# The last group of a feed-forward block's down projection: pairs 8 and 9 by Strassen's products, pair 10 into their banks, and a mixer's operands half by half

## The chip, the core and the metric

The program runs on one core of one Trainium2 chip. The metric is the device time of one execution in microseconds (us). The kernel before takes 2611.32 us, the median of 3 runs (2610.97 to 2614.04).

Five engines work side by side, each through its own stream of instructions in a fixed order: TensorE (PE; the loads of its stationary operand are shown apart, PEld), VectorE (DVE), ScalarE (ACT), GpSimd (POOL) and SyncE (SP, which issues the transfers). An instruction that waits for another engine holds up all that stand behind it on its own engine. Matmuls add into PSUM banks; the other operands lie in SBUF.

## The reference

T = 512 + 256 = 768 tokens of width 1024 pass through two layers. Each has a feed-forward block (FFN) ahead of and behind its mixer, and a last norm ends the trunk:

```python
def swiglu(h, wg, wu, wd):
    return (jax.nn.silu(h @ wg) * (h @ wu)) @ wd
...
    x = x + 0.5 * swiglu(rmsnorm(x, f1_n), f1_g, f1_u, f1_d)
    x = x + mixer_ab(rmsnorm(x, mix_n), w_in, ...)        # layer 1: mixer_c(..., w_qkv, rpb, w_out)
    x = x + 0.5 * swiglu(rmsnorm(x, f2_n), f2_g, f2_u, f2_d)
...
    return rmsnorm(x, final_norm)
```

Gate and up are 1024x2816, down is 2816x1024, all in float32. `mixer_ab` is a gated unit beside windowed attention, `mixer_c` attention within a 2-D neighbourhood.

## The kernel before

**Operands in two parts.** Every float32 factor is split into a high part, which ScalarE casts, and a low part, which VectorE forms as the factor less the high part. A product is three matmuls (`mm3`, lines 187 to 192): high by high, high by low, low by high. For weights, `wsplit` (111 to 123) writes `whi` (cast, L121) and `wlo` (subtraction, L122) into five buffers each, or, with `keep`, into two of the eight buffers of tag `s`. For activations, `split` (205 to 208) does the same (L207, L208). The weights come as `raw` tiles of 128x1024 float32, in four buffers, by transfers that SP issues in the order of the code.

**The residual** is `self.x[0..7]`: eight rows of 128 channels by 768 tokens. HALVES are tokens 0 to 383 (half 0) and 384 to 767 (half 1). Most matmuls have 384 columns, one half.

**An FFN** (`ffn`, line 475) cuts the 2816 hidden channels into 11 pairs of 128-channel blocks. `pair(p)` computes gate and up for a pair by Strassen's seven products in Winograd's form on a 2x2 cut of weights and tokens, and `hidden` ends with four quarters h11, h12, h21, h22 (block by half). `operands(q)` makes from them the seven right-hand operands b11, t1, b21, t2, t3, b22, n4 of the down projection, each split; for an odd pair the last four steps of it are kept in `self.later`, and `more(n)` takes n of them between the products of `down`.

`down(pre, pairs, d, acc)` (696) multiplies the down weights with these operands, again by seven products, for two pairs at a time: 0 and 1, 2 and 3, 4 and 5, 6 and 7. Each product goes into four banks j = 0 to 3 (128 output channels each). X, Y, Z and W name the four sums: t1 goes to Z, which is added to the four accumulators `acc`; b11 to X, copied by ScalarE into Y ("fork"); b21 ends X, added to x (rows 0 to 3, half 0); t2 goes on in Y, copied into W; t3 gives Y for rows 4 to 7, half 1; b22 ends W for rows 0 to 3, half 1; n4 ends Y for rows 4 to 7, half 0. `sums` (674) makes the four sums of weights s1 to s4 on VectorE, 128x512 each.

The eleventh pair leaves an odd one: pair 8 goes through `down` alone after pair 9's gate and up. While pair 10's gate and up run, `last_operands` (747) splits pair 9's quarters into `dh` and adds each accumulator into its two quarters of x (eight additions, L757). Then `last_operands` splits pair 10's quarters, and `down_last` (761) multiplies pairs 9 and 10 plainly: for each row m four blocks k, two halves, three matmuls, 192 matmuls in all. Its weights come as two rows' columns at a time (4 blocks by 256).

**What follows an FFN** is one of four things, so each FFN has its own tail: first FFN into mixer 0 (`m0`), second into the third FFN (`f`), third into mixer 1 (`m1`), fourth into the last norm (`last`). Where an FFN or the last norm follows (`lag`), `down_last` does half 0 of all rows first, keeps half of the weights' splits, and calls `half_done(0)` between the halves; a mixer gets both halves of a row one after the other. After each addition into x, `final` (792) squares the row for the following norm (L227, L230), and for a mixer, once half 1 of a row is there, makes `xh` (ScalarE, L806) and `xl` (VectorE, L807), the split of x times the norm's gain, which mixer 0 or 1 multiplies in the order of rows 0 to 7. For mixer 1 the tokens are reordered on the way (`columns`), which takes three pieces per row.

**What sets the order.** PE's order is that of the code. The other engines are ordered by a scheduler when the program is built, from the code's order and modelled times. Work beside the main stream (norm steps, feeding the next FFN) runs in generators that are stepped when a modelled PE time is reached; DELAY1 and the arguments of `norm_half` are such delays in us. PSUM has two pools of four banks, `ps_mm` and `ps_aux`, each used in turn.

## Time and profile before

| | before |
|---|---|
| median of 3 runs | 2611.32 us |
| the profiled execution, its time | 2610.36 us |
| its span | 2608.6 us |
| mean granted clock of TensorE | 0.993 |
| PE busy | 2561.0 us (98%), 15114 instructions |
| PEld busy | 2492.0 us (96%) |
| DVE busy | 2249.8 us (86%), 4699 |
| ACT busy | 1369.1 us (52%), 2867 |
| first matmul on `dh` in the four FFNs | 478.59, 1222.34, 1709.69, 2560.34 us |

The profile shows one execution. Busy times are sums over the span, which hides stages of different kinds; so the prediction reads stretches and single rows as well. In an instruction's row stand its start and its duration, the engine, the line of the code, output and inputs, and at the end, where there was one, the idle time before it and what ended it. The four times in the last row mark where the plain products begin, and so where the tails lie.

### The profile page before, as it was taken

What the parts mean: (1) busy time and instruction counts of PE and PEld (TensorE: products, weight loads), DVE (VectorE), ACT (ScalarE), POOL (GpSimd) and SP (SyncE); (2) the same over time, 40 slices, a digit from 0 to 9 for tenths busy, and PEclk for the clock granted to TensorE, in tenths of its full rate; (3) what the DMA queues carried; (4) which work ended last, traced back from release to release, by engine and by line L of the source; (5) the groups of instructions that cost most, each with busy time, mean ns of one, the idle gap of its engine ahead of it and who ended that gap; (6) DMA issues with size and microseconds to landing.
All of it is one profiled execution on the core that took longest, in us unless ns stands there. A gap on an engine that the chain in (4) does not pass through costs nothing.

```text
span 2608.6 us, 41165 instructions
## 1 busy us (share of the span) xinstructions
PE 2561.0 (98%) x15114; PEld 2492.0 (96%) x15114; DVE 2249.8 (86%) x4699; ACT 1369.1 (52%) x2867; POOL 89.8 (3%) x173
## 2 busy tenths in 40 slices
PE   8999999999999999999999999999999999999998
PEld 8999999988899999999999999989898999999997
DVE  8998899888779989889999888986777699888897
ACT  7544454556665545445654445454455475444543
POOL 0000000000100000000000000001222100000000
PEclk9999999999999999999999999999999999999999
DMA  6333222421223322122322222232221322222222
GB/s 217 111 115 92 80 73 65 153 71 52 81 78 97 97 65 77 70 80 83 97 81 81 76 71 73 72 129 63 64 64 40 106 91 96 81 65 81 67 68 77
DMA packets 86201, 221.87 MB, mean 85 GB/s; under 512 B 20464, under 2 KB 33264, under 8 KB 86000
## 3 DMA queue, kind: packets, MB, share of 16 engines
q1 hardware_dynamic: 85712, 218.96, 26.3%
q8 instruction: 118, 1.93, 0.3%
q14 instruction: 83, 0.68, 0.1%
q10 hardware_dynamic: 288, 0.29, 0.1%
HBM read 209.78 MB, written 15.07 MB: 86 GB/s over the span
## 4 chain that ended last, share of the span: by engine, by line
PE 86%; DVE 9%; ACT 2%; issue 1%; DMA 1%; SPq 0%; DVEq 0%; ACTq 0%
PE ps_mm L151 54%; PE ps_aux L151 31%; DVE wlo L122 2%; PE ps_aux L155 1%; DVE s L676 1%; ACT p L1005 1%; DVE xl L807 1%; DMA raw<-in_w 1%; DVE p L999 0%; DVE tl L208 0%; DVE ol L208 0%; DVE u L560 0%; ACT whi L121 0%; ACT xh L806 0%; DVE p L1015 0%
## 5 line engine op out<-in xcount | busy, mean ns | idle before, releaser
L121 ACT CAST whi<-s 128x512 fp32r<-128x512 f32 x496 | 304.8, 621 | 417.6 <-DVE s L676 186.8
L121 ACT CAST whi<-raw 128x512 fp32r<-128x512 f32 x504 | 306.1, 619 | 234.0 <-PE ps_mm L151 94.5
L122 DVE TENSOR_TENSOR wlo<-s,whi 128x512 fp32r<-128x512 f32 x496 | 336.8, 684 | 56.5 <-ACT whi L121 51.1
L122 DVE TENSOR_TENSOR wlo<-raw,whi 128x512 fp32r<-128x512 f32 x486 | 330.7, 688 | 24.0 <-ACT whi L121 17.8
L151 PE MATMUL ps_mm<-db,whi 128*128 128x384 f32 x864 | 219.3, 334 | 0.4 <-DVE sg L569 0.4
L151 PE MATMUL ps_aux<-dt,whi 128*128 128x384 f32 x864 | 219.2, 334 | 0.0
L151 PEld LDWEIGHTS ps_mm<-db,whi 128*128 128x128 f32 x864 | 156.0, 188 | 0.7 <-DVE sg L569 0.7
L151 PEld LDWEIGHTS ps_aux<-dt,whi 128*128 128x128 f32 x864 | 156.0, 188 | 0.0
L151 PE MATMUL ps_mm<-xh,whi 128*128 128x512 f32 (+1 forms) x416 | 147.9, 356 | 4.0 <-ACT xh L806 4.0
L151 PE MATMUL ps_aux<-dt,wlo 128*128 128x384 f32 x432 | 144.4, 334 | 1.4 <-DVE wlo L122 1.4
L151 PE MATMUL ps_mm<-db,wlo 128*128 128x384 f32 x432 | 144.3, 334 | 0.0
L151 PE MATMUL ps_mm<-xl,whi 128*128 128x512 f32 (+1 forms) x416 | 143.0, 344 | 1.1 <-DVE xl L807 1.1
L151 PE MATMUL ps_mm<-xh,wlo 128*128 128x512 f32 (+1 forms) x416 | 142.6, 343 | 0.0
L560 DVE TENSOR_TENSOR u<-ps_aux,u 128x384 f32<-128x384 f32 x176 | 96.8, 550 | 5.4 <-PE ps_aux L151 5.2
L676 DVE TENSOR_TENSOR s<-raw,raw 128x512 f32<-128x512 f32 x124 | 83.9, 684 | 20.3 <-DMA raw<-in_w 20.3
L676 DVE TENSOR_TENSOR s<-raw 128x512 f32<-128x512 f32 x124 | 84.8, 684 | 17.2 <-DMA raw<-in_w 17.0
L151 PE MATMUL ps_aux<-dh,whi 128*128 128x384 f32 x384 | 97.7, 335 | 0.6 <-DVE x L773 0.6
L1005 ACT ACTIVATE p<-p,st 128x256 f32<-128x256 f32 (+3 forms) x144 | 68.9, 480 | 52.8 <-DVE st L1003 52.7
L728 DVE TENSOR_TENSOR x<-ps_aux,x 128x384 f32<-128x384 f32 x160 | 84.7, 550 | 13.7 <-PE ps_aux L151 13.7
L151 PEld LDWEIGHTS ps_mm<-xh,whi 128*128 128x128 f32 x416 | 80.7, 194 | 14.4 <-ACT xh L806 4.9
L151 PE MATMUL ps_mm<-oh,whi 128*128 128x384 f32 x256 | 88.8, 347 | 4.6 <-DVE x L982 4.0
L728 DVE TENSOR_TENSOR x<-ps_mm,x 128x384 f32<-128x384 f32 x160 | 85.7, 550 | 5.8 <-PE ps_mm L151 5.6
(507 smaller groups left out, 8044.4 us busy)
## 6 DMA issues: line engine op xcount, KB each, us to landing
raw<-in_w SPq DMA_DIRECT2D x346, 512.0 KB, 3.6
xdm<-x SPq DMA_DIRECT2D x16, 384.0 KB, 2.3
x<-in_x SPq DMA_DIRECT2D x16, 192.0 KB, 4.7
tok<-in_xt SPq DMA_DIRECT2D x12, 256.0 KB, 6.3
x<-xdm SPq DMA_DIRECT2D x8, 384.0 KB, 4.2
xold<-xdm SPq DMA_DIRECT2D x8, 384.0 KB, 3.0
out_y<-y SPq DMA_DIRECT2D x8, 384.0 KB, 2.4
tab<-skew SPq DMA_DIRECT2D x8, 256.0 KB, 6.6
```

What stands on the lines that cost most here:

```text
L121: nc.scalar.copy(hi, src)
L122: (eng or nc.gpsimd).tensor_tensor(out=lo, in0=src, in1=hi.bitcast(F32), op=ALU.subtract)
L151: self.nc.tensor.matmul(out, lhsT=lhsT, rhs=rhs, start=start, stop=stop, **kw)
L155: self.nc.tensor.transpose(out, src, self.ident)
L560: nc.vector.tensor_tensor(out=t, in0=bank[key, n], in1=t, op=ALU.add)
L676: f = lambda o, x, y, op: self.nc.vector.tensor_tensor(out=o, in0=x, in1=y, op=op)
L728: nc.vector.tensor_tensor(out=o, in0=ps, in1=o, op=ALU.add)
L807: nc.vector.scalar_tensor_tensor(out=lo, in0=src, scalar=gain, in1=hi.bitcast(F32), op0=ALU.mult, op1=ALU.subtract)
L1005: ins = nc.scalar.activation(outs[i], outs[i], AF.Exp, bias=nm[:, i : i + 1], accum_out=sm[:, i : i + 1])
```

## The change

Four edits, the first by far the largest.

1. Pair 8 no longer goes through `down` alone, and pair 9 no longer through `last_operands`: pair 9's quarters become the seven Strassen operands (`operands(p - 1)`). `down_last` is written anew. It takes pairs 8 and 9 through the seven products, each product's weights split before the product ahead of it runs. Z starts from the accumulators (`seed`, four copies by ScalarE into the banks) and is then added to x twice per bank (`fifth`), instead of by eight additions of `acc`. Pair 10's plain products are added into the banks that are ending: `finish` puts two blocks, six matmuls, behind the last matmul of X in b21 (rows 0 to 3, half 0), of Y in n4 (rows 4 to 7, half 0) and of W in b22 (rows 0 to 3, half 1). Rows 4 to 7 of half 1 get banks of their own (V), which are computed ahead of each bank of b22. Pair 10's quarters are split by `operand(0)`, which stands in the code behind product b11, and `operand(1)` behind t2.
2. Pair 10's weights are loaded as two column halves of both blocks (`load_plain`); the splits of the first are kept from the start, those of the second are made before n4. Pairs 8 and 9 load four whole rows.
3. `sums` forms s1 with s1 or s2, whichever is asked for first. `down_last` asks for s2 twice, at its start and ahead of t2.
4. `final` makes xh and xl for each half as it comes, with the second half of mixer 1's tokens in the pieces 384 to 511 and 512 to 767 (`columns` gets a first row, `r0`). DELAY1 and the last norm's `norm_half` get other delays.

```diff
-DELAY1 = (26.0, 12.0)
+DELAY1 = (27.0, 14.0)
...
-                steps = operands(p - 1) if p < NPAIR - 1 else self.last_operands(dl, 0, hs[p - 1], acc)
+                steps = operands(p - 1)
...
-            if p == NPAIR - 2:
-                self.down(pre, range(p - 1, p), d, acc)
...
-        for _ in self.last_operands(dl, 2, hs[NPAIR - 1]):
-            pass
-        self.down_last(pre, dl)
+        self.down_last(pre, range(NPAIR - 3, NPAIR - 1), d, hs[NPAIR - 1], acc)
...
+        if name in ("s1", "s2") and (n, "s1") not in s:
+            t = s[n, "s1"] = self.fw.tile([P, 4, P], F32, tag="s", name="s1", bufs=8)
+            f(t, a21, a22, ALU.add)
...
+        def operand(half):
             for i in (0, 1):
...
+                dl[i, half] = self.dtile("h"), self.dtile("h")
+                self.split(*dl[i, half], h[i, half])
...
+        def fork(key, to):
+            def each(j):
+                bank[to, j] = new(to)
+                nc.scalar.copy(bank[to, j], bank[key, j])
+            return each
...
+        def finish(key, j, f, g, start=False):
+            if start:
+                bank[key, j] = new(key)
+            for k in (0, 1):
+                st = plain[f][k]
+                self.mm3(
+                    bank[key, j], (st[0][:, j, :], st[1][:, j, :]), dl[k, g], start and k == 0, k == 1, not start
+                )
+            add(key, j, f, g)
+            self.final(4 * f + j, *HALVES[g])
...
+        split_plain(0, load_plain(0))
+        for p in pairs:
+            load(p, 1)
+            load(p, 2)
+        sums("s1")
+        sums("s2")
...
+        def fifth(j):
+            for f in (0, 1):
+                add("Z", j, f, 1)
...
+        w1, w2 = split(sums("s1")), part(1, 1)
+        product(w1, "t1", "Z", fifth, seed=acc)
+        w1 = part(1, 2)
+        product(w2, "b11", "X", fork("X", "Y"), start=True)
+        more(3)
+        operand(0)
+        w2 = split(sums("s2"))
+        product(w1, "b21", "X", lambda j: finish("X", j, 0, 0))
+        more(1)
+        s3 = sums("s3")
+        w1 = split(s3)
+        product(w2, "t2", "Y", fork("Y", "W"))
+        more(3)
+        operand(1)
+        s4 = sums("s4")
+        w2 = part(2, 2)
+        r = load_plain(1)
+        product(w1, "t3", "Y", lambda j: add("Y", j, 1, 1))
+        split_plain(1, r)
+        product(w2, "n4", "Y", lambda j: finish("Y", j, 1, 0))
+        if lag:
             self.half_done(0)
...
+        product(split(s4), "b22", "W", lambda j: finish("W", j, 0, 1), ahead=lambda j: finish("V", j, 1, 1, True))
+        if lag:
             self.half_done(1)
...
-        if self.nxt[0] in ("m0", "m1") and c1 == T:
+        if self.nxt[0] in ("m0", "m1"):
...
-            for a, b in GROUPS if self.nxt[0] == "m1" else HALVES:
...
+            for a, b in ((c0, c1),) if not cols else ((H, TA), (TA, T)) if c0 else ((0, H),):
...
-            yield from self.norm_half(h)
+            yield from self.norm_half(h, 2.0, 6.0)
```

In the order of PE's stream, the third product b21 of the third FFN begins as follows in the new kernel; `db` are operands of pairs 8 and 9, `dh` pair 10's quarters, `khi` and `klo` its kept weights, and `ps_mm_18793` the bank X of row 0.

```order
L151 MATMUL ps_mm_18793<-db_18241,whi_18785 128x384
L151 MATMUL ps_mm_18793<-db_18242,whi_18785 128x384
L151 MATMUL ps_mm_18793<-db_18241,wlo_18786 128x384
L151 MATMUL ps_mm_18793<-db_18559,whi_18789 128x384
L151 MATMUL ps_mm_18793<-db_18560,whi_18789 128x384
L151 MATMUL ps_mm_18793<-db_18559,wlo_18790 128x384
L151 MATMUL ps_mm_18793<-dh,khi_18705 128x384 x2
L151 MATMUL ps_mm_18793<-dh,klo_18706 128x384
L151 MATMUL ps_mm_18793<-dh,khi_18709 128x384 x2
L151 MATMUL ps_mm_18793<-dh,klo_18710 128x384
```

Nothing stands between the sixth matmul of the product and the first on `dh`. Before, the casts of pair 10's quarters of half 0 stood on ScalarE inside pair 10's own gate and up work (the row `dh<-sg` with x2; the other rows `dh` are pair 9's, L570 is the silu):

```order
L207 CAST dh<-sg 128x384
L121 CAST whi_18826<-s_18617 128x512
L570 ACTIVATE sg<-sg 128x384
L121 CAST whi_18892<-raw_18890 128x512
L207 CAST dh<-u_18124 128x384
L207 CAST dh<-u_18209 128x384
L121 CAST whi_18911<-raw_18890 128x512
L207 CAST dh<-sg 128x384 x2
L570 ACTIVATE u_18694<-u_18694 128x384
```

Now they stand on ScalarE behind the copies of the fork (L803), which follow product b11 bank by bank, two weight casts and the cast of an operand `dt`:

```order
L803 COPY ps_aux_18800<-ps_mm_18793 128x384
L803 COPY ps_aux_18809<-ps_mm_18802 128x384
L803 COPY ps_aux_18818<-ps_mm_18811 128x384
L121 CAST whi_18854<-s_18848 128x512
L121 CAST whi_18944<-s_18940 128x512
L803 COPY ps_aux_18827<-ps_mm_18820 128x384
L207 CAST dt_18834<-u_18130 128x384
L207 CAST dh<-sg 128x384 x2
```

The two casts of the row `dh<-sg` with x2 moved from the middle of pair 10's gate and up to behind the fourth bank of b11. On VectorE, where the low parts of `dh` are made, the rows at this place are now these, with sums of weights (L672) between the two halves of `operand(0)`:

```order
L208 TENSOR_TENSOR dt_18835<-u_18130,dt_18834 128x384
L122 TENSOR_TENSOR wlo_18945<-s_18940,whi_18944 128x512
L208 TENSOR_TENSOR dh<-sg,dh 128x384
L672 TENSOR_TENSOR s_18846<-raw_18715,s_18846 128x512
L208 TENSOR_TENSOR dh<-sg,dh 128x384
L672 TENSOR_TENSOR s_18848<-raw_18719,s_18848 128x512
```

Before, low parts stood between steps of pair 10's gate and up (those on `u` are pair 9's):

```order
L122 TENSOR_TENSOR wlo_18893<-raw_18890,whi_18892 128x512
L572 SCALAR_TENSOR_TENSOR sg<-sg,v 128x384
L208 TENSOR_TENSOR dh<-u_18124,dh 128x384
L560 TENSOR_TENSOR u_18694<-ps_aux_18761,u_18694 128x384
L208 TENSOR_TENSOR dh<-u_18209,dh 128x384
L569 TENSOR_TENSOR u_18694<-u_18694,acc 128x384
L208 TENSOR_TENSOR dh<-sg,dh 128x384
```

They moved behind product b11 here as well. At the end of the third FFN, the last row's square, `xh` pieces and the mixer's first weight casts stood on ScalarE like this before (`x_8159` is the last row of the residual):

```order
L806 ACTIVATE xh_18864<-x_8153,gains 128x4x64
L121 CAST whi_19490<-raw_19488 128x512
L230 ACTIVATE sq<-x_8159 128x384
L806 ACTIVATE xh_18865<-x_8159,gains 128x8x56
L806 ACTIVATE xh_18865<-x_8159,gains 128x8x8
L806 ACTIVATE xh_18865<-x_8159,gains 128x4x64
```

and now like this, where `x_8162` is row 7 and `x_7614` row 3, the last to be finished:

```order
L121 CAST whi_19348<-raw_19342 128x512
L121 CAST whi_19354<-raw_19352 128x512
L121 CAST whi_19358<-raw_19352 128x512
L121 CAST whi_19531<-raw_19529 128x512
L230 ACTIVATE sq<-x_8162 128x384
L879 ACTIVATE xh_18694<-x_8162,gains 128x2x56
L879 ACTIVATE xh_18694<-x_8162,gains 128x2x8
L879 ACTIVATE xh_18694<-x_8162,gains 128x4x64
L230 ACTIVATE sq<-x_7614 128x384
L879 ACTIVATE xh_18690<-x_7614,gains 128x2x56
L879 ACTIVATE xh_18690<-x_7614,gains 128x2x8
L879 ACTIVATE xh_18690<-x_7614,gains 128x4x64
```

Four weight casts stand ahead of the last two rows, and the last row to be finished is row 3 instead of row 7.

More of the change, by code (lines that the diff above doesn't have):

```diff
@@ L485, in ffn @@
         acc = []
-        d, dl = {}, {}
+        d = {}
         def operands(q):
@@ L745, in down @@
         product(w["a22"], "n4", "Y", False, (1, 0))
-    def last_operands(self, d, k0, h, acc=None):
-        todo = [(j, o) for o in ((0, 1), (1, 1)) for j in range(4)] if acc else []
-        for half in (0, 1):
-            for i in (0, 1):
-                d[k0 + i, half] = self.dtile("h"), self.dtile("h")
-                self.split(*d[k0 + i, half], h[i, half])
-                yield
-                for j, (f, g) in todo[:3]:
-                    x = self.x[4 * f + j][:, HALVES[g][0] : HALVES[g][1]]
-                    self.nc.vector.tensor_tensor(out=x, in0=x, in1=acc[j], op=ALU.add)
-                    yield
-                todo = todo[3:]
@@ L787, in down_last @@
             self.half_done(0)
-            for m, st in [later[i // 2 + (0 if i % 2 else 4)] for i in range(KD)]:
-                one(m, st, 1)
+        product(split(s4), "b22", "W", lambda j: finish("W", j, 0, 1), ahead=lambda j: finish("V", j, 1, 1, True))
+        if lag:
             self.half_done(1)
@@ L880, in otile, with columns @@
         return self.xp.tile([P, T], F32, tag=f"x{k}", name=f"o{k}")
-    def columns(self, src, *dst, g):
+    def columns(self, src, *dst, g, r0=0):
         src = src.rearrange("p (r c) -> p r c", c=64)
-        dst = [t.rearrange("p (c r) -> p r c", c=64) for t in dst]
+        dst = [t.rearrange("p (c r) -> p r c", c=64)[:, r0 : r0 + src.shape[1]] for t in dst]
         if g:
```

74 lines of the change are left out of this document (48 added, 26 removed).

## The prediction

> **What bounds the kernel now.** I read the page first, its busy times and its chain of waits:
>
> ```profile
> span 2608.6 us, 41165 instructions
> PE 2561.0 (98%) x15114; PEld 2492.0 (96%) x15114; DVE 2249.8 (86%) x4699; ACT 1369.1 (52%) x2867; POOL 89.8 (3%) x173
> PE 86%; DVE 9%; ACT 2%; issue 1%; DMA 1%; SPq 0%; DVEq 0%; ACTq 0%
> ```
>
> PE sets the end almost everywhere, and VectorE is the only engine near it. So a matmul fewer is worth its slot, as long as the others deliver in time. The second view is the table by stretches: a steady one, then the last 33.2 us of matmuls of each of the four feed-forward blocks (FFNs; the plain products of pairs 9 and 10).
>
> ```profile
> core 0: us, PE busy (x) PEld busy (x) DVE busy (x) ACT busy (x) POOL busy (x), PEclk, DMA share, GB/s
> 1440.00:1480.00 40.00, 40.00 (x232) 40.00 (x232) 32.90 (x59) 18.05 (x36) 0.00 (x0) 1.00 0.21 67
> 478.60:511.80 33.20, 33.20 (x193) 33.20 (x193) 28.91 (x56) 20.83 (x41) 0.00 (x0) 1.00 0.39 135
> 1222.30:1255.50 33.20, 33.20 (x196) 33.20 (x195) 28.68 (x67) 20.53 (x42) 0.00 (x0) 1.00 0.07 23
> 1709.70:1742.90 33.20, 32.59 (x187) 32.05 (x187) 28.16 (x51) 20.12 (x38) 0.30 (x2) 1.00 0.35 123
> 2560.30:2593.50 33.20, 32.52 (x189) 31.95 (x188) 24.50 (x60) 11.17 (x22) 0.42 (x1) 1.00 0.10 36
> ```
>
> One matmul of 384 columns takes 40/232 = 0.172 us. The ends of the first and second FFN are pure PE; the third and fourth lose half a microsecond there. What follows the third, the entry to mixer 1, is another matter. The chain in order of time, and the two stretches behind it:
>
> ```profile
> 1743.34 1.08 ACT xh L806
> 1744.45 2.00 DVE xl L807 x3
> 1748.45 1.01 ACT xh L806
> 1749.49 0.83 DVE xl L807
> 1753.12 1.00 ACT xh L806
> 1754.15 1.31 DVE xl L807 x2
> 1755.50 2.50 PE ps_mm L151 x5
> 1744.00:1756.50 12.50, 7.36 (x26) 4.85 (x25) 10.62 (x20) 7.10 (x14) 0.05 (x1) 0.80 0.50 165
> 1756.50:1767.00 10.50, 10.50 (x36) 8.79 (x35) 7.25 (x27) 1.66 (x6) 6.43 (x10) 0.58 0.22 57
> ```
>
> There ScalarE and VectorE pass each row of the residual to and fro (square, xh, xl), and PE waits for the last rows. In the timeline below two 128x512 matmuls start 0.23 us apart. The first projection of the mixer, 24 of them, ends at 1756.5, that is 46.8 after 1709.7, where 192 x 0.172 + 24 x 0.23 = 38.6 would do: 8.2 us lost. Then the granted clock is 0.58 for 10.5 us.
>
> ```profile
> 1744.05 0.39 PE L151 MATMUL ps_mm<-xh,whi 128*128 128x512 f32 x1
> 1744.28 0.40 PE L151 MATMUL ps_mm<-xl,whi 128*128 128x512 f32 x1
> 1654.13 0.47 ACT L555 COPY u<-ps_mm 128x384 f32<-128x384 f32 x1
> 1654.50 0.51 ACT L207 CAST db<-sg 128x384 fp32r<-128x384 f32 x1
> 1655.33 0.51 ACT L207 CAST dt<-u 128x384 fp32r<-128x384 f32 x1
> 1655.74 0.62 ACT L121 CAST whi<-raw 128x512 fp32r<-128x512 f32 x1
> 1656.26 0.51 ACT L207 CAST db<-u 128x384 fp32r<-128x384 f32 x1
> 1675.06 0.69 DVE L122 TENSOR_TENSOR wlo<-raw,whi 128x512 fp32r<-128x512 f32 x1 [0.25 <-ACT whi L121]
> 1675.66 1.94 DVE L728 TENSOR_TENSOR x<-ps_aux,x 128x384 f32<-128x384 f32 x4
> 1677.53 1.94 DVE L728 TENSOR_TENSOR x<-ps_mm,x 128x384 f32<-128x384 f32 x4
> 1681.24 0.68 DVE L676 TENSOR_TENSOR s<-s,raw 128x512 f32<-128x512 f32 x1
> 1681.84 0.68 DVE L676 TENSOR_TENSOR s<-raw 128x512 f32<-128x512 f32 x1
> ```
>
> From these rows I take the pace of a full queue, start to start: ScalarE 0.40 for a copy or cast of 384 columns, 0.52 for a cast of 512; VectorE 0.47 for 384 (1.87/4) and 0.60 for 512. A result is there 0.08 to 0.10 later than the next start. The steps from ACT xh to DVE xl above show 0.03 us between an end and the waiting start.
>
> **The change, part by part.** Removed per FFN: pair 8 alone by Strassen was 28 groups of three matmuls, pairs 9 and 10 plainly 64. Now pairs 8 and 9 take 56 and pair 10 takes 32. That is 4 groups, 12 matmuls, 2.07 us per FFN less on PE, 8.3 us in all.
>
> VectorE, per FFN: 16 additions of 384 fewer (8 of the accumulator into x, 4 into it, 4 others), 3 more weight splits, 4 more weight sums, and 2 sums that nobody reads (s2 is formed twice), 7 more operand instructions: 9 x 0.60 + 7 x 0.47 - 16 x 0.47 = 1.2 us more. ScalarE: 4 seeds, 3 splits, 3 casts, 4.4 us more. Both lie beside PE in pair 10, where VectorE has some 4 us of 29 to spare (32.9 to 37 busy of 40 us in steady stretches); I cost them at nothing there. Were that cover gone, 1.2 us per FFN would come on top. The loads are the same bytes; one stands ahead of four others on SP, which matters only if the sums come after pair 10's last products, and by the rows of order they stand some 12 us before.
>
> Now the wait that is new. Call 0 the slot in which PE could begin product b21 (the third). Its first group of pair 10's plain product stands 6 matmuls on, at 1.03. Its operands are the two casts and two subtractions of `operand(0)`, and they stand late in both queues. ScalarE: the fourth bank of product b11 is finished at 0.16, but copies of the third bank (from -0.84) and two weight casts stand ahead of its copy; a cast dt, then the two dh follow. -0.84 + 0.40 + 2 x 0.52 = 0.60; copy to 1.00; dt to 1.41; first dh ends at 1.92, the second at 2.33. VectorE: the lower half of dt can begin at 1.55, a split of 0.60 follows, then dh from 2.62 to 3.17, a sum of 0.60, the second dh to 4.24. PE: high half waits until 1.95, low half until 3.2, and after three more slots the second operand's low half until 4.27; the group ends at 4.62 instead of 2.06. I cost this at 2.55 us per FFN. Bounds: 0, if PE is late there by that much for another reason; 4.2, if VectorE is a further 1.7 us behind (the eight additions of the product before end about then). All four tails have the same order, so it counts four times: 10.2 us. Queued behind the wait: nothing but PE's own stream; ScalarE and VectorE gain the slack.
>
> After such a stop the clock may fall. Rows of three stops:
>
> ```profile
> 676.00:684.00 8.00, 5.31 (x33) 4.60 (x33) 6.08 (x17) 7.95 (x19) 0.00 (x0) 0.95 0.00 0
> 684.00:690.00 6.00, 5.86 (x29) 4.97 (x28) 5.54 (x12) 3.07 (x8) 3.13 (x1) 0.78 0.82 261
> 757.00:762.00 5.00, 3.23 (x19) 2.90 (x18) 5.00 (x12) 2.87 (x6) 0.00 (x0) 1.00 0.00 0
> 762.00:770.00 8.00, 8.00 (x50) 8.00 (x49) 7.10 (x22) 5.40 (x11) 0.00 (x0) 1.00 0.07 25
> ```
>
> 2.7 us idle at 676 to 684 were followed by a clock of 0.78 over 6 us, and with the 0.95 before it that is 1.7 us of work lost; 1.8 us idle at 757 by none. Mine, 2.55 in three pieces, lies nearer the first. I take it in half of the first, second and fourth tail: 2.5 us (bounds 0 and 5.1). [...]
>
> The ends of the tails. First FFN (into mixer 0): two of mixer 0's weight splits now stand in both queues ahead of the last row's square, xh and xl, and this row is the fourth that the mixer multiplies, where it was the eighth. Last matmul, addition (0.8 with its queue), split 0.6, split 0.6, xh and its wait, xl: about 3.7 us, where PE comes to the fourth row after 9 x 0.23 = 2.1. Cost 1.5 (0 to 2.5). Second FFN: the next FFN starts on first-half operands that are ready early, so 0.
>
> Third FFN (mixer 1). Of a row's 2.0 us of xl in three pieces, a half has now about 1.0. The last product has 18 matmuls per bank, 3.1 us on PE; VectorE has two additions, two of the norm, two halves of xl: 4 x 0.47 + 2 x 1.0 = 3.9. Four banks put it 3.2 us behind; it comes in 2 to 3 us behind from the product before, where each row passes to and fro once, and at the end two splits are ahead. Its fourth row is ready some 8.5 us after PE's last matmul, at which PE, by 2.1, has gone through three rows: 6.4 us of waiting, in place of 8.2. The stretch at half clock stays. So halving the operands gains 1.8 us here (ends: a gain of 13.4, when the 8.2 vanishes and with it 5.2 of lowered clock, 10.5 x (1 - 0.58) = 4.4 and some 0.8 at the 0.80 before it; and a loss of 3).
>
> Fourth FFN. The first half's norm has 12.4 us of the last product to run beside (72 matmuls) instead of 16.6 (96):
>
> ```profile
> 2601.60 2.71 DVE L331 SCALAR_TENSOR_TENSOR y<-x,gains,ps_aux 128x384 f32<-128x384 f32 x5
> 2583.00:2586.00 3.00, 2.32 (x13) 1.75 (x11) 2.37 (x9) 1.46 (x4) 0.00 (x0) 1.00 0.00 0
> ```
>
> Two outputs of the first half now stand at VectorE's very end: 2 x 0.53 (2.71 less 0.07, the overrun of the last, over 5), 1.05. The wait for the norm's spread, 0.7 now, grows by about 1, since its rsqrt steps stand between additions that wait for PE. The last addition stands behind other work, 1 more. Together 3.0 (1 to 4.5).
>
> Sum: -8.3 + 10.2 + 2.5 + 1.5 + 0 - 1.8 + 3.0 = +7.1 us. The profiled execution took 2610.36, so 2617.5; the runs' median, 2611.32, lies 0.04% above it, and on that scale I say 2618.
>
> **Rivals.**
> 1. The operands come in time. If the casts were ready by 1.03, the 10.2 and the 2.5 fall away: 2611.3 + 7.1 - 12.7 = 2605.7, faster. For it: in the other down groups PE never waits behind these same copies. Against it: there nothing that is needed in the next 2 us is queued behind them. It decides in this sense below 0.5 us of wait per tail.
> 2. Mixer 1's entry comes clear: VectorE does its halves while PE still multiplies. 8.2 lost and 5.2 of lowered clock vanish instead of 1.8: 2618.4 - 11.6 = 2606.8. Against it the 3.9 beside 3.1 us per bank.
> [...]
> 4. VectorE drags: with 1.2 us per FFN uncovered, 4.2 instead of 2.55 per stop and a lowered clock in each: 4.8 + 6.6 + 2.5 more than forecast, taken at two thirds: 2628.
> 5. The change doesn't do what it says: the splits a product ahead are undone by the five buffers of each half. Against it, the rows of order hold the split order; its cost is inside 4.
>
> **How the numbers follow.** Forecast 0.40 (2612 to 2625 as its own range); rival 1 0.17; rival 2 0.10; rival 3 0.15; rival 4 with 5 0.18. Range from rival 1 with a little of 2, 2603, to rival 4, 2628. A measurement of this kernel tells 0.2%, 5.2 us, from no change. Slower by more: most of the forecast and rival 4, 0.55. Within: rival 3, half of 2 and the forecast's low end, 0.25. Faster: rival 1 and half of 2, 0.20.
>
> **What would show it.** Right: about 15032 matmuls where there were 15080 in the program; in each tail a group of matmuls on dh in the third product that waits first for ACT dh, then twice for DVE dh, 2 to 3 us in all; waits on xh and xl in the fourth row at 1745 to 1760 and about 500; VectorE's last rows y behind the second half's. Wrong: no waits for dh above 0.5 us; a clock of 1.00 behind mixer 1's entry; PE idle in pair 10, which would mean that its cover was thinner than I took it.

## The result, and the profile after

| | before | after |
|---|---|---|
| median of 6 runs each | 2613.72 us | 2626.86 us |
| their spread | 2610.97 to 2615.91 | 2622.36 to 2632.33 |
| ratio, 95% interval | | 1.0054 (1.0039 to 1.0069) |
| the profiled execution | 2610.36 | 2625.20 |

The change makes the kernel slower by 0.54%, some 13 to 14 us; the forecast was 2618 in 2603 to 2628. The page of the changed kernel, its busy times and its chain of waits:

```profile
span 2623.4 us, 41169 instructions
PE 2561.6 (98%) x15066; PEld 2485.2 (95%) x15066; DVE 2256.2 (86%) x4715; ACT 1387.3 (53%) x2923; POOL 91.0 (3%) x173
PE 84%; DVE 11%; ACT 3%; issue 1%; DMA 1%; DVEq 0%; SPq 0%; ACTq 0%
```

PE has 48 instructions fewer (15114 to 15066) and yet the same busy time, which means that some matmuls ran longer; and the chain goes over VectorE for 11% where it was 9%. Where the 14.8 us between the two spans came in is best seen by setting the same matmul of both streams side by side. "Later by" is the start after less the start before.

| at | before | after | later by | growth |
|---|---|---|---|---|
| FFN 1, behind the group of pairs 6 and 7 | 405.79 | 406.02 | 0.2 | 0.2 |
| mixer 0, first matmul | 511.87 | 514.27 | 2.4 | **2.2** (first tail) |
| FFN 2, first matmul | 766.81 | 771.23 | 4.4 | 2.0 |
| FFN 2, behind pairs 6 and 7 | 1149.54 | 1154.31 | 4.8 | 0.4 |
| FFN 3, first matmul | 1256.29 | 1263.09 | 6.8 | **2.0** (second tail) |
| FFN 3, behind pairs 0 and 1 | 1383.13 | 1392.52 | 9.4 | 2.6 |
| FFN 3, behind pairs 6 and 7 | 1636.89 | 1646.28 | 9.4 | 0 |
| mixer 1, first matmul | 1744.05 | 1754.19 | 10.1 | **0.8** (third tail) |
| FFN 4, first matmul | 2104.57 | 2116.00 | 11.4 | 1.3 |
| FFN 4, behind pairs 6 and 7 | 2487.54 | 2500.07 | 12.5 | 1.1 |
| the last norm's first sum on PE | 2595.88 | 2609.43 | 13.5 | **1.0** (fourth tail) |
| end of the span | 2608.6 | 2623.4 | 14.8 | 1.3 |

"Growth" is what came in since the row above; a tail is the end of an FFN from the group of its last pairs on, an entry the first matmuls of the part behind it. Each tail should have been 2.07 us shorter. What it met instead, in the third FFN, on ScalarE, VectorE and PE in turn (the timeline of each engine):

```profile
1713.45 0.47 ACT L803 COPY ps_aux<-ps_mm 128x384 f32<-128x384 f32 x1
1713.86 0.50 ACT L207 CAST dt<-u 128x384 fp32r<-128x384 f32 x1
1714.26 0.92 ACT L207 CAST dh<-sg 128x384 fp32r<-128x384 f32 x2
...
1714.39 0.56 DVE L208 TENSOR_TENSOR dt<-u,dt 128x384 fp32r<-128x384 f32 x1 [0.23 <-ACT dt L207]
1714.87 0.68 DVE L122 TENSOR_TENSOR wlo<-s,whi 128x512 fp32r<-128x512 f32 x1
1715.47 0.55 DVE L208 TENSOR_TENSOR dh<-sg,dh 128x384 fp32r<-128x384 f32 x1
1715.94 0.68 DVE L672 TENSOR_TENSOR s<-raw,s 128x512 f32<-128x512 f32 x1
1716.54 0.55 DVE L208 TENSOR_TENSOR dh<-sg,dh 128x384 fp32r<-128x384 f32 x1
...
1713.71 0.34 PE L151 MATMUL ps_mm<-db,wlo 128*128 128x384 f32 x1
1714.82 0.45 PE L151 MATMUL ps_mm<-dh,khi 128*128 128x384 f32 x1 [0.78 <-ACT dh L207]
1716.08 0.44 PE L151 MATMUL ps_mm<-dh,khi 128*128 128x384 f32 x1 [0.81 <-DVE dh L208]
1716.36 0.47 PE L151 MATMUL ps_mm<-dh,klo 128*128 128x384 f32 x1
1716.63 1.21 PE L151 MATMUL ps_mm<-dh,khi 128*128 128x384 f32 x2
1717.14 0.29 PEld L151 LDWEIGHTS ps_mm<-dh,khi 128*128 128x128 f32 x1 [0.50 <-DVE dh L208]
1717.63 0.52 PE L151 MATMUL ps_mm<-dh,klo 128*128 128x384 f32 x1
```

PE stops for the first cast of `dh`, then for each of the two low parts; the stop for the second low part shows on the weight load (PEld), within PE's row with x2. The first bank of b21, twelve matmuls that need 2.07 us, takes 2.69 us more than that in the first and fourth tail (in the second and third, where the clock falls within it, 3.03). The table by stretches shows what the clock did: two stretches of 3.41 us for each of the four tails, the one with the stop and the next.

```profile
core 0: us, PE busy (x) PEld busy (x) DVE busy (x) ACT busy (x) POOL busy (x), PEclk, DMA share, GB/s
473.95:477.36 3.41, 1.72 (x7) 1.14 (x8) 3.23 (x6) 1.80 (x5) 0.00 (x0) 1.00 0.00 0
477.36:480.78 3.42, 3.42 (x12) 3.42 (x11) 2.18 (x5) 1.84 (x4) 0.00 (x0) 0.50 0.00 0
1221.47:1224.88 3.41, 1.82 (x8) 0.94 (x6) 3.22 (x7) 2.57 (x7) 0.00 (x0) 1.00 0.02 5
1224.88:1228.30 3.42, 3.14 (x11) 3.13 (x11) 2.85 (x6) 1.49 (x4) 0.00 (x0) 0.50 0.00 0
1712.99:1716.40 3.41, 1.82 (x10) 1.25 (x9) 3.19 (x6) 3.02 (x8) 0.00 (x0) 1.00 0.03 7
1716.40:1719.82 3.42, 3.42 (x11) 2.92 (x10) 2.78 (x6) 1.04 (x2) 0.00 (x0) 0.50 0.00 0
2566.32:2569.73 3.41, 1.95 (x10) 1.38 (x8) 3.27 (x8) 3.41 (x8) 0.00 (x0) 1.00 0.02 5
2569.73:2573.15 3.42, 3.01 (x16) 2.69 (x17) 3.25 (x8) 1.04 (x4) 0.00 (x0) 1.00 0.00 0
```

In three of four tails the granted clock is 0.50 in the following stretch. Counted over 72 matmuls from the start of b21, the tails lose 4.29, 4.15, 3.95 and 2.73 us, 15.1 in all; that is more than the whole difference, and the saving of 8.3 goes against it. The rest of the growth lies at the entries. Mixer 0 waits for its fourth row (PE's timeline):

```profile
517.15 0.50 PE L151 MATMUL ps_mm<-xh,whi 128*128 128x512 f32 x1 [0.63 <-ACT xh L879]
518.22 0.50 PE L151 MATMUL ps_mm<-xl,whi 128*128 128x512 f32 x1 [0.57 <-DVE xl L880]
```

At mixer 1's entry (the table by stretches) PE has 4.66 us of work in 10.8, while VectorE is busy for 10.61 of them, and the clock falls once more:

```profile
1754.20:1765.00 10.80, 4.66 (x13) 2.16 (x13) 10.61 (x27) 9.20 (x24) 0.00 (x0) 0.80 0.78 260
1762.50:1769.30 6.80, 5.73 (x16) 4.25 (x17) 5.84 (x13) 0.90 (x3) 3.99 (x4) 0.62 0.88 260
```

Mixer 1's four long waits for xh and xl (PE's timeline), first before, then after:

```profile
1749.67 0.50 PE L151 MATMUL ps_mm<-xh,whi 128*128 128x512 f32 x1 [1.34 <-ACT xh L806]
1750.91 0.50 PE L151 MATMUL ps_mm<-xl,whi 128*128 128x512 f32 x1 [0.74 <-DVE xl L807]
1754.33 0.80 PE L151 MATMUL ps_mm<-xh,whi 128*128 128x512 f32 x1 [2.69 <-ACT xh L806]
1755.50 0.79 PE L151 MATMUL ps_mm<-xl,whi 128*128 128x512 f32 x1 [0.37 <-DVE xl L807]
...
1757.83 0.50 PE L151 MATMUL ps_mm<-xh,whi 128*128 128x512 f32 x1 [1.55 <-ACT xh L879]
1759.12 0.50 PE L151 MATMUL ps_mm<-xl,whi 128*128 128x512 f32 x1 [0.79 <-DVE xl L880]
1762.80 0.79 PE L151 MATMUL ps_mm<-xh,whi 128*128 128x512 f32 x1 [2.94 <-ACT xh L879]
1764.36 0.79 PE L151 MATMUL ps_mm<-xl,whi 128*128 128x512 f32 x1 [0.77 <-DVE xl L880]
```

FFN 3 starts with VectorE behind. PE's first stop there is at the 37th matmul, which begins the fourth bank of `ps_mm`; by the order of the banks that is the one from which VectorE's last addition of the tail (L808) still had to read. The profile names `yl`, which ended just behind that addition. The 49th matmul waits for ScalarE's copy `p` (the timelines of VectorE and of PE):

```profile
1269.20 0.55 DVE L808 TENSOR_TENSOR x<-ps_mm,x 128x384 f32<-128x384 f32 x1
1269.90 0.41 PE L151 MATMUL ps_mm<-b110h,whi 128*128 128x384 f32 x1 [0.41 <-DVE yl L295]
1273.15 0.44 PE L151 MATMUL ps_mm<-b210h,whi 128*128 128x384 f32 x1 [0.91 <-ACT p L585]
```

At the end VectorE has six outputs in a row (its timeline) where it had five:

```profile
2614.94 3.24 DVE L331 SCALAR_TENSOR_TENSOR y<-x,gains,ps_aux 128x384 f32<-128x384 f32 x6 [0.55 <-ACT acc L908]
```

### The profile page after: what moved, and what is told of

It is laid out like the page before. It is cut to its first block, busy times and chain, and to the rows that moved or that the text cites. A ratio compares the mean times of both kernels' runs of the same rounds, so it can differ in the third digit from the quotient of the medians.

```text
span 2623.4 us, 41169 instructions
## 1 busy us (share of the span) xinstructions
PE 2561.6 (98%) x15066; PEld 2485.2 (95%) x15066; DVE 2256.2 (86%) x4715; ACT 1387.3 (53%) x2923; POOL 91.0 (3%) x173
## 4 chain that ended last, share of the span: by engine, by line
PE 84%; DVE 11%; ACT 3%; issue 1%; DMA 1%; DVEq 0%; SPq 0%; ACTq 0%
PE ps_mm L151 54%; PE ps_aux L151 29%; DVE wlo L122 2%; DVE s L672 1%; PE ps_aux L155 1%; ACT p L1078 1%; DVE p L1072 0%; DVE tl L208 0%; DVE x L808 0%; DVE xl L880 0%; ACT whi L121 0%; DMA raw<-in_w 0%; DVE p L1088 0%; DVE acc L234 0%; DVE u L560 0%
## 5 line engine op out<-in xcount | busy, mean ns | idle before, releaser
L122 DVE TENSOR_TENSOR wlo<-s,whi 128x512 fp32r<-128x512 f32 x512 | 347.5, 684 | 58.2 <-ACT whi L121 52.5
L151 PE MATMUL ps_mm<-db,whi 128*128 128x384 f32 x960 | 245.5, 336 | 0.0
L151 PE MATMUL ps_aux<-dt,whi 128*128 128x384 f32 x960 | 243.5, 334 | 0.0
L151 PEld LDWEIGHTS ps_mm<-db,whi 128*128 128x128 f32 x960 | 174.9, 189 | 0.0
L151 PEld LDWEIGHTS ps_aux<-dt,whi 128*128 128x128 f32 x960 | 173.4, 188 | 0.0
L151 PE MATMUL ps_aux<-dt,wlo 128*128 128x384 f32 x480 | 160.4, 334 | 1.4 <-DVE wlo L122 1.4
L151 PE MATMUL ps_mm<-db,wlo 128*128 128x384 f32 x480 | 161.4, 336 | 0.0
L672 DVE TENSOR_TENSOR s<-raw,raw 128x512 f32<-128x512 f32 x128 | 86.3, 684 | 21.6 <-DMA raw<-in_w 21.1
L672 DVE TENSOR_TENSOR s<-raw 128x512 f32<-128x512 f32 x128 | 87.6, 685 | 18.1 <-DMA raw<-in_w 18.0
L672 DVE TENSOR_TENSOR s<-s,raw 128x512 f32<-128x512 f32 x136 | 92.6, 683 | 0.7
L570 ACT ACTIVATE sg<-sg 128x384 f32<-128x384 f32 x88 | 46.3, 526 | 86.6 <-DVE sg L569 86.2
L151 PEld LDWEIGHTS ps_aux<-dt,wlo 128*128 128x128 f32 x480 | 90.1, 188 | 1.8 <-DVE wlo L122 1.8
```

The costliest lines, as they stand in the source:

```text
L122: (eng or nc.gpsimd).tensor_tensor(out=lo, in0=src, in1=hi.bitcast(F32), op=ALU.subtract)
L151: self.nc.tensor.matmul(out, lhsT=lhsT, rhs=rhs, start=start, stop=stop, **kw)
L570: nc.scalar.activation(t, t, AF.Silu)
L672: f = lambda o, x, y, op: self.nc.vector.tensor_tensor(out=o, in0=x, in1=y, op=op)
```

## Experiments

Ratios are against the kernel before, run beside each experiment on the same chip; a difference between two experiments is taken between their ratios, times 2611 us.

**1 and 2. Is it the place of `dh` in the queues?** The first experiment brings the operand forward, the second makes PE come to it later and moves nothing else by intent.

```diff
+        operand(0)
         product(w2, "b11", "X", fork("X", "Y"), start=True)
         more(3)
-        operand(0)
```

> operand(0) is written ahead of product b11 instead of behind it, so that the casts and low parts of pair 10's quarters of half 0 come earlier in the queues. Theory (the operand is late in the queues): in the changed kernel the first bank of b21 loses 2.7 us per tail (the row spacings at 1222.85 and on), 10.7 in all, and 1.6 us of half clock behind it in three tails, 4.8; both vanish, 2626.9 - 15.5 = 2611. Rival (VectorE drags): the wait only moves to the operands dt and the additions that are pushed back, and at most half comes back: 2618 to 2624. A wait on dh below 0.3 us with a time above 2618 would speak for the rival.

```diff
-        product(w1, "b21", "X", lambda j: finish("X", j, 0, 0))
+        product(w1, "b21", "X")
+        for j in range(4):
+            finish("X", j, 0, 0)
```

> Nothing moves on ScalarE or VectorE by intent: b21 first does the 24 matmuls of pairs 8 and 9 for all four banks, and only then the 24 of pair 10, so PE comes to dh 3.1 us later. Theory: the last low part of dh is ready 3.2 us after PE needs it first and 2.2 after it needs the second block, so the wait all but vanishes (0 to 0.5 per tail) and the half clock with it: 2611 to 2613. Rival (VectorE drags): the four additions and the feeding of rows 0 to 3 now come in a bunch at the product's end, and the gain is given back there: 2618 to 2624.

| | median | ratio | against after |
|---|---|---|---|
| dh_early | 2613.57 | 1.0004 (0.9996 to 1.0013) | 13.1 us better |
| dh_behind_banks | 2615.08 | 1.0007 (0.9999 to 1.0016) | 12.3 us better |

Two quite different edits give the same. The loss over the 72 matmuls is 0.2 us per tail in the first and 0.05 or less in the second, against 2.7 to 4.3. What the trace says dh_early should bring, 15.1 - 0.8 = 14.3, and what the ratios say, 13.1, lie 1.2 us apart. The medians are 2 to 3 us above what was expected, and below the rivals' 2618 to 2624. So the slowdown is the stop and the half clock behind it, and without it the change is even with the kernel before, not 8.3 us better.

**3. A smaller dose.** Here `operand(0)` stays behind b11, and goes ahead of one operand of t3 only.

```diff
-        more(3)
+        more(1)
         operand(0)
+        more(2)
```

> The changed kernel with operand(0) still behind product b11, but ahead of the operand dt of t3: on ScalarE the casts of dh stand one cast earlier, on VectorE their low parts one subtraction and one split earlier. Theory (the stop is the place in the queues, and the clock falls after a window of 3.41 us in which PE was busy for about half): the stop of 2.68 us falls by 1.1 to some 1.6 per tail, such a window is then busy for 0.55 or more and the half clock follows in at most one of the four: 2626.9 - 4.4 - 3.2 = 2619 (2616 to 2621). Rival (the clock falls after any stop of a microsecond): the clock stays low in three of four and the time is 2622 to 2623.

Measured: 2621.84 us, ratio 1.0025 (1.0014 to 1.0036). The four stops are 1.62 us each, as expected to 0.1, and no tail has a half clock; the first and second, with the stretch behind each:

```profile
474.00:477.41 3.41, 2.60 (x13) 1.72 (x12) 3.13 (x7) 2.87 (x7) 0.00 (x0) 1.00 0.00 0
477.41:480.83 3.42, 3.42 (x21) 3.42 (x20) 3.23 (x8) 1.60 (x4) 0.00 (x0) 1.00 0.02 5
...
1225.00:1228.41 3.41, 2.60 (x13) 1.72 (x12) 3.28 (x7) 2.54 (x7) 0.00 (x0) 1.00 0.02 7
1228.41:1231.83 3.42, 3.42 (x21) 3.42 (x21) 3.42 (x8) 2.08 (x5) 0.00 (x0) 1.00 0.00 0
```

By the stops this kernel stands 6.6 - 0.8 = 5.8 us behind dh_early, and by the ratios 5.5. The median itself lies 0.8 us above the range that was given for it, in the rival's direction, but what the rival claimed, a low clock in three of four tails, isn't there.

**4 and 5. What are the halves worth?** One kernel has the change without them, the other the halves without the change. For the first:

```diff
-        if self.nxt[0] in ("m0", "m1"):
+        if self.nxt[0] in ("m0", "m1") and c1 == T:
...
-            for a, b in ((c0, c1),) if not cols else ((H, TA), (TA, T)) if c0 else ((0, H),):
+            for a, b in GROUPS if self.nxt[0] == "m1" else HALVES:
```

> The changed kernel with the old final: a mixer's xh and xl are made for a row when its half 1 is there, not half by half. Theory (the end of a tail into a mixer is bound by VectorE and ScalarE): the low parts of half 0 (8 rows, about 1.0 us each for mixer 1, 0.5 for mixer 0) come into the last product of 12.4 us, the entry to mixer 1 is 6 to 8 us later and that to mixer 0 3 to 4: 2636 to 2639. Rival (the halves do not matter, since the wait there is one of latency between the two engines): 2625 to 2629.

> The kernel before with the new final alone (xh and xl half by half), nothing of the down group changed. Theory (VectorE and ScalarE bind the end of these tails): half of the last rows' pieces is done while PE multiplies, the 6.3 us of waits at 1745 to 1755 fall by 2 to 4 and the stretch of half clock may shorten: 2613.7 - 3 = 2610.7 (2606 to 2613). Rival (latency between the engines, which halving does not shorten): 2613 to 2615.

| | median | ratio |
|---|---|---|
| rows_whole | 2627.84 | 1.0061 (1.0048 to 1.0073) |
| halves_alone | 2612.97 | 1.0000 (0.9991 to 1.0009) |

The first theory fails: the halves are worth 0.07%, 1.8 us, with the change, inside the intervals. For the halves alone the median of 2612.97 stands at the edge of both ranges; the ratio of 1.0000 speaks for the rival, and so does the trace, in which mixer 1's four long gaps between starts, each less the usual 0.23, add up to 6.8 us (6.3 before) and the half clock lasts 13.65 us as before. In the trace of rows_whole mixer 1's first projection ends 3.1 us later than in the changed kernel, not 6 to 8, and mixer 0's entry is the same. In this trace, too, three of four tails have the half clock, but the first, second and third of the changed kernel are here the second, third and fourth: six of eight such stops were followed by it.

**6 and 7. Do the entries give it back, and can they be cleared?** Both build on dh_early. One sets W ahead of V in the last product, so that row 7 and not row 3 is ready last:

```diff
-        product(split(s4), "b22", "W", lambda j: finish("W", j, 0, 1), ahead=lambda j: finish("V", j, 1, 1, True))
+        def ends(j):
+            finish("W", j, 0, 1)
+            finish("V", j, 1, 1, True)
+
+        product(split(s4), "b22", "W", ends)
```

> dh_early, with W of a row ahead of V in the last product (rows 0, 4, 1, 5, 2, 6, 3, 7 in place of 4, 0, 5, 1, 6, 2, 7, 3). Theory (a mixer waits on row 3, which is ready last, with four of eight rows still behind it): the 1.65 us of waits at mixer 0's start vanish, and at mixer 1 the 12 to 16 matmuls that stood behind the last operand now stand ahead of it, 2.8 to 4 us; 2613.6 - 5 = 2609 (2607 to 2611). Rival (VectorE's queue ends at the same time and PE waits for row 7 as it did for row 3): 2612 to 2615.

The other spreads the work of half 1 over two products:

```diff
-        product(w2, "n4", "Y", lambda j: finish("Y", j, 1, 0))
+        def fourth(j):
+            finish("Y", j, 1, 0)
+            if j:
+                finish("V", j - 1, 1, 1, True)
+
+        product(w2, "n4", "Y", fourth)
...
+        finish("V", 3, 1, 1, True)
+        product(split(s4), "b22", "W", lambda j: finish("W", j, 0, 1))
...
+READY = 4, 5, 6, 7, 0, 1, 2, 3
...
+        pkv = [(self.proj(wk, xs, GROUPS[g], ks=READY), self.proj(wv, xs, GROUPS[g], ks=READY)) for g in (0, 1)]
```

> dh_early, with V (rows 4 to 7, half 1) one bank behind Y within product n4 instead of ahead of each bank of b22, and the mixers' first projections in the order of rows 4 to 7, 0 to 3. Theory (what the tails gave back is VectorE's work for half 1, squeezed into the last 12.4 us): the work of eight rows is spread over 16.6 us, the wait at the entry of the third FFN (2 to 3 us), at mixer 0 (1.65) and part of that at mixer 1 (2 to 5) vanish: 2613.6 - 8 = 2606 (2603 to 2609). Rival (VectorE has the same sum to do and is behind anyway; V waits for the banks of Y): 2611 to 2616.

| | median | ratio |
|---|---|---|
| row7_last | 2612.25 | 1.0002 (0.9992 to 1.0011) |
| v_in_n4 | 2613.73 | 1.0001 (0.9993 to 1.0010) |

By the measured time both fail; the traces show why. In row7_last mixer 0's 1.65 us are gone and mixer 1's first projection gains 2.6, but FFN 3 starts with one gap of 2.75 us between matmul starts where dh_early had two of 0.74 and 1.25, and the last norm has one of 2.30. In v_in_n4 mixer 0 gains 1.65, FFN 3's entry 0.8 and mixer 1 more, but the third tail gets a new stop of 2.0 us with a half clock behind it, since the low part of s4 now stands behind the rows' work on VectorE (PE's timeline; one line was added above, so `mmul` is L152):

```profile
1736.08 0.45 PE L152 MATMUL ps_mm<-db,wlo 128*128 128x384 f32 x1 [1.66 <-DVE wlo L123]
```

and the last norm ends 1.5 us later.

**8 and 9. Smaller suspects.** Old delays in dh_early, and s2 formed once in dh_early:

```diff
-DELAY1 = (27.0, 14.0)
+DELAY1 = (26.0, 12.0)
...
-            yield from self.norm_half(h, 2.0, 6.0)
+            yield from self.norm_half(h)
```

> dh_early with the delays of the kernel before (DELAY1 26 and 12, the last norm's 1.8 and 4). Theory (the third FFN's entry and the last norm lose by VectorE's backlog, not by where the norm's steps stand): 2612.5 to 2615. Rival (the norm's steps stand at the wrong places): 2 us or more either way.

```diff
-        sums("s2")
+        s2 = sums("s2")
...
-        w2 = split(sums("s2"))
+        w2 = split(s2)
```

> dh_early without the second forming of s2 (two sums of 0.60 us per FFN that nobody reads). Theory (they lie beside PE in pair 10's gate and up): 2613 to 2614. Rival (VectorE is the bound there and what it does more comes on top): 8 x 0.60 = 4.8 less, 2609.

| | median | ratio |
|---|---|---|
| delays_before | 2617.33 | 1.0018 (1.0008 to 1.0028) |
| s2_once | 2613.17 | 1.0008 (0.9999 to 1.0018) |

The two idle sums cost nothing, as costed: they do lie beside PE. The delays of before are worse by 0.14% in the new kernel, 3.7 us, as the rival had it, though the two intervals overlap. Its runs reach from 2610.49 to 2621.93 us and the profiled one took 2610.78, so the trace need not hold what the others lose; this stays open.

**10. A version ahead of both kernels.** v_in_n4 in the three tails ahead of a mixer or an FFN, dh_early's order in the last, s2 once, and the split of s4 ahead in the queues:

```diff
+        spread = self.following[0] != "last"
...
-            if j:
+            if j and spread:
...
+        with self.tc.high_priority():
+            w4 = split(s4)
```

> v_in_n4 in the three tails ahead of a mixer or an FFN, dh_early's order in the last tail, s2 formed once, and the split of s4 set ahead in the queues. Theory (VectorE's backlog at the end of a tail sets the entry to what follows): as in v_in_n4 the waits at mixer 0 (1.65) and 4.6 us at mixer 1 are gone, and now also the 2.0 us stop on the low part of s4 at 1734 with its half clock (1.7) and the 2 us that the last norm lost there; 2613.6 - 1.65 - 4.6 = 2607 (2604 to 2609). Rival (what is cleared at one place comes back as the next wait): 2611 to 2614.

Measured: 2609.95 us, ratio 0.9986 (0.9977 to 0.9995): faster than the kernel before by 0.14%, and by 0.68% than the changed one. The expected 2607 was 3 too low, and the median lies between the two ranges. Its profiled execution:

```profile
span 2603.5 us, 41155 instructions
PE 2551.9 (98%) x15066; PEld 2482.5 (95%) x15066; DVE 2250.5 (86%) x4707; ACT 1386.7 (53%) x2923; POOL 91.1 (3%) x173
```

PE's busy time is 9.1 us less than before, near the 8.3 that the matmuls should bring. That alone proves little: this execution took 2605.29 us, 4.7 below its median, and dh_early, whose time did not fall, has 2554.5 us of PE. The trace also shows where the expected gain went. At mixer 1's third matmul PE now waits for the low part of the first weights (PE's timeline), a place where dh_early has no such wait:

```profile
1742.20 0.50 PE L152 MATMUL ps_mm<-xh,wlo 128*128 128x512 f32 x1 [3.55 <-DVE wlo L123]
```

That is the rival's mechanism: what is cleared at one place comes back as the next wait. Three kinds of tail were changed at once, so which of the edits brings how much was not taken apart.

**11 and 12. Is VectorE the bound at the entries?** The running sum of squares (L234) was first moved to GpSimd, then left out, in dh_early. Both edits hit the norms behind the mixers too, five norms with 70 additions; the expectations speak of the tails alone.

```diff
-            nc.vector.tensor_tensor(out=self.acc[:, a:b], in0=self.acc[:, a:b], in1=sq, op=ALU.add)
+            eng = nc.vector if self.nxt[0] == "last" else nc.gpsimd
+            eng.tensor_tensor(out=self.acc[:, a:b], in0=self.acc[:, a:b], in1=sq, op=ALU.add)
```

> dh_early with the norm's running sum of squares (L234, 16 additions per tail, 0.47 us each on VectorE) on GpSimd in all tails but the last. Theory (VectorE bounds the ends of the tails and the first 100 us of the third FFN): 7.5 us of its work per tail are gone, the waits at the entry of FFN 3 (2 us) and mixer 0 (1.65) vanish and those at mixer 1 shrink by 2.5 or more: 2613.6 - 6 = 2607 (2605 to 2610). Rival (the waits are latency from engine to engine, and GpSimd, with 1.0 us for such an addition, makes the norm later): 2612 to 2617.

> dh_early without the running sums of squares (the 16 additions L234 of a tail) in all tails but the last; this part of the norm is not computed, so that the scale is that of the first row's squares alone. Theory (VectorE bounds the ends of these tails and the first 100 us of FFN 3): 7.5 us less on VectorE per tail, the entry to FFN 3 loses its waits (2 us), mixer 0 its 1.65 and mixer 1 some 3: 2613.6 - 6.5 = 2607 (2604 to 2609); what it is better than the run with these additions on GpSimd is what the two engines took from each other, some 19. Rival (latency between engines): 2612 to 2614.

| | median | ratio |
|---|---|---|
| sums_on_pool | 2625.88 | 1.0052 (1.0039 to 1.0066) |
| sums_left_out | 2599.94 | 0.9943 (0.9930 to 0.9955) |

Leaving 70 additions of 0.47 us away, 33 us of VectorE, brings 15.9 us against dh_early, and nothing was taken from PE. The additions also stand on the path of the norms that read them, so the total does not tell a full VectorE from a shorter path. Two places do. The operands xh and xl of mixer 1, and the bank that FFN 3's 37th matmul waits for, do not read the sums; yet mixer 1's four long gaps, each less 0.23, fall from 7.0 to 4.9 us in sum, and the stop at the 37th matmul is gone. There VectorE's queue is the bound. In the two profiled executions, 10.6 us apart, 3.2 us come in FFN 3's first two pairs and 4.9 between the first matmuls of mixer 1 and FFN 4; how much of the whole is the norms' path was not separated. The first 100 us of FFN 3 in the table by stretches (columns as above), first the kernel before, then dh_early, then the one without the sums:

```profile
1256.30:1356.30 100.00, 100.00 (x580) 99.97 (x580) 95.73 (x194) 57.57 (x118) 0.00 (x0) 1.00 0.37 116
```

```profile
1255.85:1355.85 100.00, 97.38 (x556) 95.43 (x556) 94.22 (x200) 57.09 (x118) 0.00 (x0) 1.00 0.33 106
```

```profile
1252.40:1352.40 100.00, 99.63 (x577) 99.31 (x576) 95.69 (x201) 58.05 (x120) 0.00 (x0) 1.00 0.35 113
```

PE was just covered before (100.00) with VectorE at 95.73 of 100; in the new order it waits 2.6 us, and with VectorE relieved 0.4. On GpSimd the same additions make it 28 us slower than leaving them out (26 between the medians), where 19 was expected; what can be said of the reason is told below.

## Why the prediction was right or wrong

It was right on the side and on the main cause, and short of the size: +7.1 us were forecast, and the medians lie 13.1 us apart, the two profiled executions 14.8. The measured 2626.86 lies inside the stated range of 2603 to 2628, but near its end and outside the forecast's own 2612 to 2625. That end came from rival 4, of whose three terms only the clock comes near what was found (uncovered work in pair 10: nothing; a stop of 4.2 us: 2.69; a lowered clock in each tail: in three of four). That its 2628 is the nearest number is luck.

- **12 matmuls less per FFN, -8.3.** Right: 48 fewer. With the stop removed (dh_early) the first three tails are 1.9 to 2.3 us shorter than before, as 2.07 says.
- **The new stop, 2.55 us four times.** Right in place, order of waits and size: 2.69 four times, and 1.62 where a smaller dose was forecast at 1.6. Rival 1 (the operands come in time) falls.
- **The clock, 2.5 us ("half of the first, second and fourth tail").** Mis-sized: three of four, 1.60, 1.46 and 1.26 us over the stop alone, 4.3 in all. Rival 3 (the stops leave the clock alone, 2615.9) falls by these three; PE's longest gap between starts in the four stops was 1.25 us. What goes with the half clock is the busy share of the stretch of 3.41 us with the stop: 0.50 to 0.57 in the four tails, and 0.76 at the smaller dose, where the clock stayed. The third tail, which the forecast left out, had it, and the fourth, which it counted, had none.
- **Mixer 0, 1.5.** Right: 1.65 us, on xh and xl of the fourth row; row7_last, in which this row is not last, has no such wait.
- **FFN 3's entry: "the next FFN starts on first-half operands that are ready early, so 0".** This step failed: 2.6 us. The operands were early enough (the first 36 matmuls ran without a wait), but VectorE was full (95.7 of 100 us before), the change squeezes half 1's work from 16.6 us into 12.4, and the bank of its last addition came free too late. VectorE's 86% on the page of the profile hid this, and my "32.9 to 37 busy of 40" came from a calmer stretch. "I cost them at nothing there" held for pair 10, where s2_once shows it, but not behind it: rival 4's mechanism at a smaller size.
- **Mixer 1, -1.8 by "halving the operands".** Wrong. The norm's first spread there comes 0.4 us less late than the first matmul; the sum of its four long gaps, less 0.23 each, rose from 6.3 to 7.2 us while the half clock, which was said to stay, shrank from 13.65 to 6.83. What the halves are worth, 1.8 us with the change and nothing without it, cannot be told from noise; that the one equals the forecast's 1.8 is no proof of it. The step left out a cost. A half takes about 1.0 us at VectorE's pace, as said, but a row now has five pieces instead of three: over this tail the pieces of xl add up to 21.1 us on VectorE where they were 17.3, those of xh to 22.9 on ScalarE where they were 18.2. VectorE is what is short there (10.61 of 10.80 us busy, and shorter waits in sums_left_out), and the halves give it more to do.
- **The last norm, 3.0.** Mis-sized within its bounds (1 to 4.5): 1.3 at the end and 0.4 in the tail beyond the stop, 1.7.
- **Not in the sum.** Third tail 1.1 us better than stop and saving say; one more stretch of half clock at mixer 1's end (2109) and small delays in FFN 4's start and mixer 0, 3.2 us together. Such stretches lie at different places in the traces of kernels that do not differ there (in mixer 0 at 581, 632 and 683 us before, at 633 and 684 in dh_early), so I can't lay them to the change.
- **Two slips of the working.** "Rows of three stops" shows two, at 676 and 757. And the 0.8 us of lowered clock ahead of 1756.5 is part of the 8.2, so that the gain of 13.4 and rival 2's price count it twice. Neither enters the sum.

The terms of the profiled execution then are -8.3 + 10.8 + 4.3 + 1.65 + 2.6 - 0.4 + 1.7 - 1.1 + 3.2 = 14.4, of 14.8.

## What to carry to other kernels

An operand that is made late costs at the place where PE first needs it (2.69 us in each tail here); before moving work, walk both producing queues to that place and add up what stands ahead, and if it is late, let PE do other banks first: dh_behind_banks took three lines. Taking 12 matmuls out of a tail shortened the first three by 1.9 to 2.3 us in dh_early, and FFN 3's entry, where VectorE was busy for 95.7 of 100 us before, lost 2.6 in the changed kernel: so read VectorE's share in the stage and the 100 us behind it, not over the whole span. Cutting a row into five pieces instead of three to start earlier gave the engines more to do (xl 21.1 us where it was 17.3, xh 22.9 where it was 18.2), and VectorE was the one that was short there (10.61 of 10.80 us): set such an increase against what the earlier start gains, here 1.8 us that cannot be told from noise. And a stop can be charged again by the clock: six of eight stops like the 2.69 us here were followed by the half clock (1.26 to 1.60 us more in the changed kernel's three), those of 1.62 us in none of four.

## What the runs showed of the hardware

**In these traces the clock goes by stretches of 3.41 us.** Every change of the granted clock in the 14 profiles lies on a grid of 3.413 us, and each low stretch is one to four such steps long. I took all steps at full clock in which PE was busy for less than 80% (from 130 us after the start to 15 us before the end), with the clock of the next step (a matmul's row lasts 0.33 us where its slot is 0.17, so the busy share is on the high side):

| busy share of the step | steps | next step at half clock |
|---|---|---|
| below 0.45 | 26 | 26 |
| 0.45 to 0.55 | 33 | 20 |
| 0.55 to 0.60 | 35 | 10 |
| 0.60 to 0.80 | 131 | 11 |

The grid's position differs from run to run, so the same stop falls into one step or is shared by two: the fourth tail's 2.7 us left its step busy for 1.95 of 3.41 us and went free. A step that was half busy (0.45 to 0.55) was followed by the half clock in 20 of 33 cases.

**Beside GpSimd's additions three steps of VectorE took longer.** In sums_on_pool GpSimd did three additions from 2109.25 to 2113.0, and three of VectorE's steps on 128x3 elements, 0.16 us each when alone, took 0.80 to 0.99 in that time (the timelines of GpSimd and of VectorE):

```profile
2109.25 3.75 POOL L235 TENSOR_TENSOR acc<-acc,sq 128x384 f32<-128x384 f32 x3
```

```profile
2110.04 0.80 DVE L318 TENSOR_SCALAR smi<-sm 128x3 int32<-128x3 int32 x1
2110.95 0.99 DVE L324 TENSOR_SCALAR sm<-sm 128x3 f32<-128x3 f32 x1
2112.04 0.98 DVE L327 TENSOR_TENSOR sm<-sm 128x3 f32<-128x3 f32 x1
2113.26 0.16 DVE L326 TENSOR_TENSOR sm<-sm 128x3 f32<-128x3 f32 x1
```

These three steps ended within 0.03 us of the ends of the three additions (2110.81, 2111.91 and 2113.00). VectorE's additions from PSUM into x took no longer (0.546 us on the mean in the 45 that ran beside these additions, 0.549 in the 363 others). Why these three, the traces do not show. In all, the 4645 VectorE instructions that both kernels have add up to 10.7 us more in sums_on_pool than in sums_left_out, likely one reason why relief by GpSimd made the kernel slower. GpSimd's own 1.2 us per addition on the norms' paths is another; what each has of the 28 us was not measured apart.
